# Two more column pairs in layer 1's front, attention steps at half quarters, conditioning spread in layer 0

## The chip, the cores and the metric

The kernel runs on one core of a Trainium2 chip. The metric is the device time of one execution in microseconds. The version before has a median of 2278.35 us over three runs (2276.54 to 2283.84).

The engines go by their names in the profile: PE is TensorE (PEld its weight loads), DVE is VectorE, ACT is ScalarE, POOL is GpSimd, SP is SyncE, which here only issues DMAs.

## The reference: what is computed

Two layers of a diffusion trunk over 640 tokens, 512 latent and 128 context ones, model width 2048. For each layer:

```
h = rmsnorm(x) * (1 + scale) + shift          # shift, scale, gate = silu(cond) @ ada_w + ada_b
p = h @ w_in                                  # split into columns, see below
y = concat(branch1 * silu(gate1), branch2 * silu(gate2))
x = x + gate * (y @ w_out)
```

Layer 0 has windowed attention with a sink and a gated width-3 convolution. Layer 1 has *differential* attention (four heads, two softmax maps each, `cq`, `ck`, `cv`, gates `cg`) and *dense* attention (eight query heads over two key/value heads, `dq`, `dk`, `dv`, gates `dg`). Queries and keys are normalised per head, and for latent tokens rotated. Latent queries see 256 cached keys as well. New keys and values of the context tokens are outputs (`new_d_k`, `new_d_v` for the dense branch). The conditioning `silu(cond) @ ada_w` is a product with two columns (context and latent).

## The kernel before, in words

**Matrix products.** Activations lie transposed, 16 blocks of 128 rows by 640 tokens. All big products are done in three parts, high x high, high x low and low x high, of operands split into a rounded part and its remainder (`split`, L291: ScalarE copies the high part, L292; VectorE subtracts, L293). A *column tile* is 128 output columns over the 640 tokens, two halves of 320. `proj_q` (L320) does one *quarter* of it, four row blocks: 4 x 3 x 2 = 24 matmuls (L327 to L329), first half `pa`, then half `pb`.

**Column pairs.** `run_pairs` (L519) takes two column tiles together, with a two-by-two block scheme of seven products instead of eight (M1, M5, M6, M2, M7, M3, M4 in this order). Each product is half a tile's rows by half its tokens: 8 row blocks x 3 = 24 matmuls (L612 to L614, PSUM tile `pq`), so a pair has 168, and two tiles have 192. It needs sums of weight blocks (VectorE, L551 to L563) and of activations (`forms`, L1133, made once per stage and kept as `T`). There are two `slot` calls in each product, one after its first half and one at its end.

**Slots.** `run_tiles` (L379) goes through a list of jobs, each a column tile and the function that takes its result. Weights are loaded five quarters ahead (`RAW_AHEAD`) and split three ahead (`SPLIT_AHEAD`). After each quarter comes one `slot` (L367), which gives one step to each of the generators in `prep` (what is done with finished tiles: `q_gen` L723, `k_gen` L656, `v_gen` L770), `steps` steps to the first generator in `attn` (attention, or `forms`), and `rate` steps to the `fill` generator (conditioning products on VectorE). So the source writes the order by hand; the builder may still move an instruction among those of its engine where its operands allow, and allots buffers from pools.

**Attention steps.** `pair_gen` (L878 is its product with the values) works on two heads and five blocks of 128 queries, in twelve steps: a score with its softmax (L827 to L829 into `S`; L789 to L796; normalising L890), the transposes of an earlier block's weights (L815), and their product with the values. The one `S` tile takes two PSUM banks. `diff_gen` (from L1527) has fourteen steps per head.

**Conditioning.** Layer 0's conditioning partly runs on TensorE. The rest are the multiply-adds of `ada_wide` (L258), `ada_slow` (L270, L279, L281; loads by POOL into one place in `tables`) and `ada_on_dve` (L206, L216, L218; loads by SP). Each ends in a fold on TensorE (`ada_fold`, L224). `fill0b`, an `ada_slow` over two blocks of 512 columns, runs at 0.33 steps a slot in layer 0's pairs; a step is one weight tile, two multiply-adds. `fill1`, an `ada_on_dve` over four blocks in halves of 256 columns, runs at 1.3 steps a slot in layer 1's tiles.

**Order of stages.** Layer 0: lead tiles and 28 tiles with windowed attention; six more tiles from `n_turn` on, beside which `forms` runs at 0.4 steps a quarter; nine pairs of the convolution's columns. Then the output projection. Layer 1's *front*: six gate tiles, then eight pairs (eight gates, eight `cv` tiles), whose results go to DRAM (`gdram`, `vdram`; `value_rows`, L1625, turns values into rows). Then the pool `odd` opens and 30 tiles follow: dense attention's queries, keys and values (12 jobs, at one step a quarter), differential queries and keys (16, at 1.1 steps from job 13 on), and two gates. Then the output projection.

Of the kernel before, what the change touches and what calls it, by code (L numbers as in the profile page):

```python
# [11 lines left out]
F32 = mybir.dt.float32  # L12
# [8 lines left out]
P = 128  # L21
# [30 lines left out]
FILL1 = 1.3  # L52
# [4 lines left out]
def trunk_kernel(ctx: ExitStack, tc: tile.TileContext, I: dict, O: dict):  # L57
# [133 lines left out]
    def ada_on_dve(blocks, tags, parts=1, tie=lambda: None):  # L191


        wt, wd = tags[2:5], 512 // parts
        bufs = 3 if wt[0] == wt[1] else 1
        for l, cb in blocks:
            ap = pools["cur"]
            acc = [ap.tile([P, 512], F32, tag=tags[c], name=f"acc{c}", bufs=1) for c in range(2)]
            mark = tie()
            if mark is not None:  # L200
                for c in range(2):
                    V.tensor_copy(acc[c][:, 0:1], mark)
            def fetch(i):
                kt, c0 = i % KT, cb * 512 + i // KT * wd
                w = ap.tile([P, wd], F32, tag=wt[i % 3], name="adaw", bufs=bufs)
                nc.sync.dma_start(w, I["ada_w"][l, kt * P:(kt + 1) * P, c0:c0 + wd])  # L206
                return w

            nxt = fetch(0)
            for i in range(KT * parts):  # L210
                kt, h = i % KT, i // KT
                w, nxt = nxt, (fetch(i + 1) if i + 1 < KT * parts else None)
                for c in range(2):
                    a = acc[c][:, h * wd:(h + 1) * wd]
                    if kt == 0:
                        V.tensor_scalar(a, w, sT[:, kt, c:c + 1], None, ALU.mult)  # L216
                    else:
                        V.scalar_tensor_tensor(out=a, in0=w, scalar=sT[:, kt, c:c + 1], in1=a,  # L218
                                               op0=ALU.mult, op1=ALU.add)
                yield  # L220
            ada_fold(l, cb, acc, ap, tags[5], 3 if tags[5] == wt[0] else 1)
            yield
# [42 lines left out]
    def ada_slow(blocks):  # L265

        w = tables[:, 3 * HALF:3 * HALF + 512]

        def fetch(l, cb, kt):
            nc.gpsimd.dma_start(w, I["ada_w"][l, kt * P:(kt + 1) * P, cb * 512:(cb + 1) * 512])  # L270

        fetch(*blocks[0], 0)
        yield
        for b, (l, cb) in enumerate(blocks):
            acc = [xr_tile(f"acc{c}")[:, 0:512] for c in range(2)]
            for kt in range(KT):
                for c in range(2):
                    if kt == 0:
                        V.tensor_scalar(acc[c], w, sT[:, kt, c:c + 1], None, ALU.mult)  # L279
                    else:  # L280
                        V.scalar_tensor_tensor(out=acc[c], in0=w, scalar=sT[:, kt, c:c + 1], in1=acc[c],  # L281
                                               op0=ALU.mult, op1=ALU.add)
                if kt + 1 < KT:
                    fetch(l, cb, kt + 1)
                elif b + 1 < len(blocks):
                    fetch(*blocks[b + 1], 0)
                yield
# [78 lines left out]

    def slot(fill=None, rate=0.0, steps=1.0):  # L367
        settle_late()
        advance(prep, len(prep))
        pace[0] += steps  # L370
        while pace[0] >= 1.0:
            advance(attn, 1)
            pace[0] -= 1.0
# [5 lines left out]
    def run_tiles(jobs, w_ap, make_h, fill=None, rate=0.0, ahead=None, order=(0, 1, 2, 3), before=None,  # L379
# [89 lines left out]
        for i in range(lead, len(jobs)):  # L469
            fn = jobs[i][1]  # L470
            if turn and i == turn[0]:
                drain(prep)
                turn[1]()
                rate = 0.0
# [13 lines left out]
            for qd in range(4):  # L488
                proj_q(pp, parts[t], qd, qd, HV[:1] if split_last else HV)
# [7 lines left out]
                slot(fill, rate if t > fill_from else 0.0, steps(i))  # L497
# [21 lines left out]
    def run_pairs(cols, w_ap, mov, room, used, begin, done, tail, fill=None, rate=0.0):  # L519
# [82 lines left out]
        for i, (p, name) in enumerate(seq):  # L602
# [5 lines left out]
            for h in range(2):  # L608
# [7 lines left out]
                if h == 0:  # L616
                    ahead(2 * i + 1)
                    slot(fill, rate)
# [11 lines left out]
            slot(fill, rate)  # L630
# [25 lines left out]
    def k_gen(ap, pp, tag, src, gain, new_out, vals=None, then=None):  # L656
# [9 lines left out]
        x = stage(ap, pp)  # L666
# [5 lines left out]
        junk = ap.tile([P, P * st["sets"]], F32, tag="junk", name="junk", bufs=1)[:, 0:P]  # L672
# [22 lines left out]
        V.tensor_mul(y, x, cosR[:, :, None, :].to_broadcast([P, 8, 2, 32]))  # L695
# [1125 lines left out]
```

## Time and profile before

| | |
|---|---|
| median of three runs | 2278.35 us |
| the profiled execution, its time | 2275.12 us |
| its span (first to last instruction) | 2273.3 us |
| PE, DVE, ACT, POOL busy | 98%, 75%, 49%, 10% of the span |
| mean granted clock of TensorE | 0.996 |
| moved by DMA | 351.43 MB, mean 155 GB/s |

"Busy" joins the spans of an engine's instructions. A matmul's span is a model, longer than its share of the array, so busy does not mean at its peak. A wait row reads: who, of which line, waited for which engine's tile and line; then us in all, times, and the longest. A row of the stage table (from:to, length) gives busy us and count for each engine. The chain of work that ended last has 50% on PE, 6% on DVE, 3% on ACT.

### The profile page before, as it was taken

Reading aid. Unit: us, or ns where it says so; the run is one execution under the profiler, and the core shown is the slowest. Engines: PE = TensorE matmul, PEld = TensorE weight load, DVE = VectorE, ACT = ScalarE, POOL = GpSimd, SP = SyncE. Lnnn points to the kernel's source line nnn. Section 1 sums busy time; section 2 is a strip of 40 time slices with the busy share of each in tenths; the row PEclk is TensorE's granted clock in tenths of the full one; section 3 lists DMA queues with packets and bytes.
Section 4 is the critical chain, followed back from the end, with each engine's and each line's share of the span. In section 5 each row is a group of like instructions: output and inputs, shape, how many; then the busy total and the mean of one; then the engine's idle time right before and its main releaser. Section 6 shows DMA issues by size and latency. Waiting matters only on the chain.

```text
span 2273.3 us, 41407 instructions
## 1 busy us (share of the span) xinstructions
PE 2230.9 (98%) x15708; PEld 2156.4 (95%) x15708; DVE 1712.6 (75%) x3197; ACT 1109.6 (49%) x2293; POOL 225.3 (10%) x337
## 2 busy tenths in 40 slices
PE   7999999999999999999999999999999999999999
PEld 5889999999999999999999999999999999999999
DVE  4659899988868898887776764858658778676665
ACT  4335554544333435444644445566665554554443
POOL 2220000000001000000200000010010111111010
PEclk9999999999999999999999999999999999999999
DMA  9985556564534447743763334423324234237541
GB/s 357 340 284 156 175 171 204 164 188 151 157 100 130 135 122 227 210 140 113 246 211 115 108 110 141 132 71 99 94 76 145 76 115 131 78 114 245 168 134 49
DMA packets 385607, 351.43 MB, mean 155 GB/s; under 512 B 18162, under 2 KB 342224, under 8 KB 384896
## 3 DMA queue, kind: packets, MB, share of 16 engines
q1 hardware_dynamic: 369008, 289.76, 42.5%
q0 software_dynamic: 15536, 56.80, 7.2%
q8 instruction: 123, 2.02, 0.4%
q10 hardware_dynamic: 864, 2.23, 0.3%
q14 instruction: 76, 0.62, 0.1%
HBM read 305.86 MB, written 42.86 MB: 153 GB/s over the span
## 4 chain that ended last, share of the span: by engine, by line
PE 50%; DVE 6%; ACT 3%; issue 2%; DMA 2%; POOL 1%; ACTq 0%; DVEq 0%; POOLq 0%; SPq 0%
PE pq L612 8%; PE pq L613 8%; PE pq L614 8%; PE pb L328 3%; PE pb L327 3%; PE pa L329 3%; PE pb L329 3%; PE pa L328 3%; PE pa L327 3%; DVE acc L218 1%; PE T L642 1%; PE T L815 1%; DMA adaw<-in_ada_w 1%; DVE nm L789 1%; ACT p L796 1%
## 5 line engine op out<-in xcount | busy, mean ns | idle before, releaser
L292 ACT ACTIVATE wh<-raw 128x512 fp32r<-128x512 f32 (+1 forms) x400 | 241.1, 604 | 393.5 <-PE pb L328 277.3
L327 PE MATMUL pa<-h,wh 128*128 128x320 f32 x1216 | 388.7, 320 | 0.4 <-DVE sum L416 0.4
L328 PE MATMUL pa<-h,wh 128*128 128x320 f32 x1216 | 379.0, 312 | 1.5 <-DVE h L293 1.5
L327 PE MATMUL pb<-h,wh 128*128 128x320 f32 x1216 | 378.1, 311 | 0.9 <-ACT h L292 0.9
L329 PE MATMUL pa<-h,wl 128*128 128x320 f32 x1216 | 377.9, 311 | 0.0
L329 PE MATMUL pb<-h,wl 128*128 128x320 f32 x1216 | 377.8, 311 | 0.0
L328 PE MATMUL pb<-h,wh 128*128 128x320 f32 x1216 | 377.4, 310 | 0.0
L293 DVE TENSOR_TENSOR wl<-raw,wh 128x512 fp32r<-128x512 f32 (+1 forms) x400 | 261.2, 654 | 142.2 <-ACT wh L292 126.5
L612 PE MATMUL pq<-h,wh 128*128 128x320 f32 x896 | 277.4, 310 | 0.0
L614 PE MATMUL pq<-h,wl 128*128 128x320 f32 x896 | 277.1, 309 | 0.0
L613 PE MATMUL pq<-h,wh 128*128 128x320 f32 x896 | 276.6, 309 | 0.0
L327 PEld LDWEIGHTS pa<-h,wh 128*128 128x128 f32 x1216 | 228.9, 188 | 10.6 <-issue 9.7
L328 PEld LDWEIGHTS pa<-h,wh 128*128 128x128 f32 x1216 | 229.3, 189 | 6.5 <-issue 4.5
L327 PEld LDWEIGHTS pb<-h,wh 128*128 128x128 f32 x1216 | 229.5, 189 | 2.1 <-ACT h L292 1.1
L329 PEld LDWEIGHTS pa<-h,wl 128*128 128x128 f32 x1216 | 228.8, 188 | 1.6 <-issue 1.6
L328 PEld LDWEIGHTS pb<-h,wh 128*128 128x128 f32 x1216 | 229.4, 189 | 0.4 <-issue 0.4
L329 PEld LDWEIGHTS pb<-h,wl 128*128 128x128 f32 x1216 | 229.2, 188 | 0.4 <-issue 0.4
L612 PE MATMUL pq<-T,wh 128*128 128x320 f32 x672 | 209.3, 311 | 3.4 <-ACT wh L292 1.8
L614 PE MATMUL pq<-T,wl 128*128 128x320 f32 x672 | 208.3, 310 | 2.7 <-DVE wl L293 2.7
L613 PE MATMUL pq<-T,wh 128*128 128x320 f32 x672 | 208.2, 310 | 0.0
L258 DVE SCALAR_TENSOR_TENSOR acc<-adaw,sT,acc 128x1024 f32<-128x1024 f32 x150 | 189.1, 1275 | 0.0
L292 ACT ACTIVATE wh<-sx 128x512 fp32r<-128x512 f32 x168 | 105.1, 632 | 151.7 <-PE pq L613 96.2
(375 smaller groups left out, 4682.7 us busy)
## 6 DMA issues: line engine op xcount, KB each, us to landing
adaw<-in_ada_w SPq DMA_DIRECT2D x80, 512.0 KB, 4.0
raw<-in_od_w_in SPq DMA_DIRECT2D x160, 256.0 KB, 3.0
raw<-in_ev_w_in SPq DMA_DIRECT2D x130, 256.0 KB, 3.5
ada<-in_ada_w SPq DMA_DIRECT2D x11, 2048.0 KB, 13.5
adaw<-in_ada_w SPq DMA_DIRECT2D x128, 128.0 KB, 2.4
w<-in_ev_w_in SPq DMA_DIRECT2D x27, 512.0 KB, 3.9
w<-in_od_w_in SPq DMA_DIRECT2D x24, 512.0 KB, 4.0
adah<-in_ada_w SPq DMA_DIRECT2D x20, 512.0 KB, 9.2
```

Source lines behind the costliest of these rows:

```text
L218: V.scalar_tensor_tensor(out=a, in0=w, scalar=sT[:, kt, c:c + 1], in1=a, op0=ALU.mult, op1=ALU.add)
L258: V.scalar_tensor_tensor(out=acc[c], in0=w, scalar=sT[:, kt, c:c + 1], in1=acc[c], op0=ALU.mult, op1=ALU.add)
L292: A.activation(hi, x, AF.Copy)
L293: V.tensor_sub(lo, x, hi)
L327: PE.matmul(ps, wh[:, i, :], hi[:, sl], start=(j == js[0] if alone else (pos == 0 and j == 0)), stop=False)
L328: PE.matmul(ps, wh[:, i, :], lo[:, sl], start=False, stop=False)
L329: PE.matmul(ps, wl[:, i, :], hi[:, sl], start=False, stop=(j == js[1] - 1 if alone else (pos == 3 and j == 3)))
L612: PE.matmul(ps, wh[:, j, :], hi, start=(first and h == 0 and j == 0), stop=False, skip_group_check=True)
L613: PE.matmul(ps, wh[:, j, :], lo, start=False, stop=False, skip_group_check=True)
L614: PE.matmul(ps, wl[:, j, :], hi, start=False, stop=(final and h == 1 and j == 3), skip_group_check=True)
L642: PE.transpose(t[:, i * P:(i + 1) * P], src(b), ident)
L789: V.tensor_reduce(nm, s, axis=AX.X, op=ALU.max, negate=True)
```

## The change

- `dk` and `dv` (two tiles each) leave the odd stage's job list and are appended to the front as two more pairs, ahead of `cv`: `key_out` copies a key tile to SBUF and stores it in `kdram`; values go the way of `cv`, `value_rows`, to `vdram` and `new_d_v`.
- In the odd stage `keys_first` reads both key tiles back and runs `k_gen` on them, two steps a slot, beside the first tile. `with_values` loads and splits the dense values ahead of a pair's first step.
- `pace_attn`: half of a quarter's attention steps are now counted after the first half (`pa`) of the quarter, the other half at its end. Dense queries' and the next tiles (jobs 2 to 9) run at 1.5 steps a quarter, later ones at 1.1.
- `ada_slow` yields after each multiply-add instead of two, keeps two loads ahead (in `w8` tiles, later in two alternating places), starts in the six tiles of layer 0 at 0.7 steps a slot, and in the pairs moves only in the products M6, M2 and M3, one step a slot.
- `ada_on_dve` works on 512 columns instead of 256, with two buffers instead of three; `FILL1` goes from 1.3 to 0.85.
- Two scratch tiles (`junk`) become bf16, and a small tile of the lambda computation is reused.

```diff
-FILL1 = 1.3
+FILL1 = 0.85
...
     def ada_slow(blocks):
-        w = tables[:, 3 * HALF:3 * HALF + 512]
-        def fetch(l, cb, kt):
+        todo = [(l, cb, kt) for l, cb in blocks for kt in range(KT)]
+        places, ws = [], []
+        def fetch():
+            if not todo:
+                return
+            l, cb, kt = todo.pop(0)
+            if "adaw" in st:
+                w = st["adaw"]()
+            else:
+                if not places:
+                    places.extend([tables[:, 3 * HALF:3 * HALF + 512], xr_tile("adaw")[:, 0:512]])
+                w = places[0]
+                places.reverse()
             nc.gpsimd.dma_start(w, I["ada_w"][l, kt * P:(kt + 1) * P, cb * 512:(cb + 1) * 512])
...
+                    if c:
+                        ws.pop(0)
+                        fetch()
+                    yield
...
+    def pace_attn(steps):
+        pace[0] += steps
+        while pace[0] >= 1.0:
+            settle_late()
+            advance(attn, 1)
+            pace[0] -= 1.0
...
-                proj_q(pp, parts[t], qd, qd, HV[:1] if split_last else HV)
+                if split_last:
+                    proj_q(pp, parts[t], qd, qd, HV[:1])
+                else:
+                    proj_q(pp, parts[t], qd, qd, HV[:1])
+                    pace_attn(steps(i) / 2)
+                    proj_q(pp, parts[t], qd, qd, HV[1:])
...
-                slot(fill, rate if t > fill_from else 0.0, steps(i))
+                slot(fill, rate if t > fill_from else 0.0, steps(i) / 2)
...
-                    slot(fill, rate)
+                    slot(fill, float(name in rests))
...
+    def with_values(values, ap, width, k, *rest):
+        rows_, src = values
+        raw = ap.tile([P, 5, P], F32, tag="ctxv", name="vrow", bufs=1)
+        ctx_ = ap.tile([P, 2, P], F32, tag="ctxk", name="vctx", bufs=1)
+        nc.sync.dma_start(raw.rearrange("p b f -> p (b f)"), rows_)
+        nc.sync.dma_start(ctx_, src.rearrange("(c p) d -> p c d", p=P))
+        yield
+        hi, lo = st["v"] = tuple(ap.tile([P, 7, P], F32R, tag=t, name=t) for t in ("vh", "vl"))
+        split(hi[:, 2:7, :], lo[:, 2:7, :], raw)
+        split(hi[:, 0:2, :], lo[:, 0:2, :], ctx_)
+        yield from pair_gen(ap, width, k, st["v"], *rest)
...
-                     turn=(n_turn, tail_turn), twist=twist, fill_from=FILL0_FROM)
+                     turn=(n_turn, fill0b, 0.7, tail_turn), twist=twist, fill_from=FILL0_FROM)
...
-              fill0b, 0.33)
+              fill0b, ("M6", "M2", "M3"))
...
+    def key_out(j):
+        x = xr_tile("kx")
+        def put(t, sl, src):
+            A.copy(x[:, sl], src)
+            if (j, "k") in half_done:
+                nc.gpsimd.dma_start(kdram[j], x)
+            half_done.add((j, "k"))
+        return put
...
-            + [OD["cv"] + i * P for i in range(8)], N_FRONT, h1_maker,
+            + [OD[n] + i * P for n, m in (("dk", 2), ("dv", 2), ("cv", 8)) for i in range(m)], N_FRONT, h1_maker,
...
-        if n % 2 == 0:
-            jobs.append((OD["dk"] + kv * P, k_job(f"k{kv}", I["cache_d_k"][0, 0, kv], "d_k_norm", O["new_d_k"][0, 0, kv])))
-            jobs.append((OD["dv"] + kv * P, v_job(I["cache_d_v"][0, 0, kv], O["new_d_v"][0, 0, kv], then)))
+        jobs.append((OD["dq"] + (h + 1) * P, q_job("q1", "d_q_norm", then)))
+    def keys_first():
+        for kv in range(2):
+            yield from k_job(f"k{kv}", I["cache_d_k"][0, 0, kv], "d_k_norm", O["new_d_k"][0, 0, kv])(kdram[kv])
...
-    brisk.update((i, 1.1) for i in range(13, len(jobs)))
+    brisk.update((i, 1.5 if i < 10 else 1.1) for i in range(2, len(jobs)))
```

More of the change, by code (lines that the diff above doesn't have):

```diff
@@ L629, in run_pairs @@
                 tail(name)
-            slot(fill, rate)
+            slot(fill, float(name in rests))
     def stage(ap, pp):
@@ L665, in k_gen @@
         nc.sync.dma_start(raw, src.rearrange("(c p) d -> p c d", p=P))
-        x = stage(ap, pp)
+        if isinstance(pp, tuple):
+            x = stage(ap, pp)
+        else:
+            x = ap.tile([P, NT], F32, tag="stg", name="kx", bufs=2)
+            nc.sync.dma_start(x, pp)
         if vals:
@@ L928, in trunk_kernel @@
     fill0b = ada_slow([(1, 2), (1, 3)])
[L929 to L930 removed]
+    fill1 = ada_on_dve([(1, cb) for cb in range(8, 12)])
     ydram = [dram.tile([P, NT], F32, name=f"yd{k}") for k in range(KT)]
     x0dram = [dram.tile([P, 4 * NT + 1], F32, name=f"x0d{g}") for g in range(4)]
+    kdram = [dram.tile([P, NT], F32, name=f"kd{k}") for k in range(2)]
     xdram, hdram, gdram, vdram = ([dram.tile([P, NT], F32, name=f"{n}{k}") for k in range(KT)]
@@ L1512, in odd_start @@
         V.tensor_reduce(ls, lp, axis=AX.X, op=ALU.add)
-        le = small.tile([P, 2], F32, tag="le", name="le", bufs=1)
+        le = ls
         A.activation(le, ls, AF.Exp)
```

87 lines of the change are left out of this document (42 added, 45 removed).

## The prediction

> **What bounds the kernel now.** I read the head of the page first, then TensorE's timeline, the table by stage, and the waits.
>
> ```profile
> span 2273.3 us, 41407 instructions
> ...
> PE 2230.9 (98%) x15708; PEld 2156.4 (95%) x15708; DVE 1712.6 (75%) x3197; ACT 1109.6 (49%) x2293; POOL 225.3 (10%) x337
> ```
>
> TensorE is the bound, but the 0.31 us that a matmul shows is not its price, since neighbours overlap. The price is the distance of two starts. In the timeline of one quarter of a column tile:
>
> ```profile
> 600.62 0.31 PE L327 MATMUL pa<-h,wh 128*128 128x320 f32 x1
> ...
> 604.14 0.31 PE L327 MATMUL pa<-h,wh 128*128 128x320 f32 x1
> ```
>
> From the first row to the second lie 24 matmuls (four row blocks, three products, two halves) and 3.52 us: **0.1467 us each**. A quarter is 3.52 us, half a quarter 1.76, a column tile (96 matmuls) 14.08.
>
> Then by stage. First TensorE's pair products alone, in layer 0's nine pairs and in layer 1's eight front pairs:
>
> ```profile
> 653.30:887.00 233.70, 226.44 (x1512) 0.99 0.45 134
> 1188.60:1389.40 200.80, 198.62 (x1344) 1.00 0.36 108
> ```
>
> Then all engines (PE, PEld, DVE, ACT, POOL busy; granted clock, DMA share, GB/s), in the six tiles ahead of layer 0's pairs, in those pairs, and in the odd stage's start, its dense attention, and the start of differential attention:
>
> ```profile
> 562.20:653.30 91.10, 91.10 (x630) 89.89 (x629) 65.24 (x114) 31.80 (x55) 3.24 (x6) 1.00 0.44 131
> 653.30:887.00 233.70, 227.56 (x1534) 223.98 (x1534) 203.18 (x327) 100.60 (x179) 18.83 (x35) 0.99 0.45 134
> 1389.40:1462.00 72.60, 71.45 (x493) 69.76 (x492) 48.47 (x108) 31.06 (x70) 7.93 (x10) 1.00 0.54 166
> 1462.00:1690.00 228.00, 225.85 (x1604) 217.76 (x1604) 149.08 (x328) 148.41 (x296) 16.97 (x17) 1.00 0.28 85
> 1690.00:1755.00 65.00, 61.89 (x432) 60.18 (x431) 50.08 (x119) 32.78 (x79) 6.72 (x9) 0.97 0.45 136
> ```
>
> The front pairs are clean: 1344 x 0.1467 = 197.2 of 200.8 us, and the other 3.6 hold the values' transposes. Layer 0's pairs are not: 1512 x 0.1467 = 221.8 of 233.7 us. I estimate 2 us for the 22 matmuls of the conditioning folds (1534 less 1512), which leaves **9.9 us lost**. TensorE's waits there (all four rows: us, times, longest), and the longest of VectorE's, say by what:
>
> ```profile
> PE pq L614 <- DVE wl L293: 2.7, 3, 1.3
> PE pq L612 <- ACT wh L292: 1.8, 3, 0.9
> PE pq L612 <- ACT tables L581: 1.0, 1, 1.0
> PE pq L612 <- DVE tables L591: 0.6, 1, 0.6
> ```
>
> ```profile
> DVE acc L281 <- DMA tables<-in_ada_w: 18.7, 19, 2.2
> ```
>
> VectorE is 87% busy there (203.18 of 233.70) and besides sits 18.7 us waiting for conditioning weights, in front of the splits that TensorE needs. TensorE's rows name 6.1 of the 9.9 us; the rest I put to the clock (1% of 233.7 us is 2.3) and short gaps.
>
> **The change part by part.**
>
> *Four tiles become two pairs.* Removed: 4 x 96 = 384 tile matmuls. Added: 2 x 168 = 336 pair matmuls. 48 x 0.1467 = **7.0 us less**, which nothing can hide, since TensorE is without slack in both stages. The transposes of keys and values and the copies out of PSUM are as many as before. The two new pairs should lose as little as the eight beside them: VectorE and ScalarE have room there, and if not, 9.9 / 9 = 1.1 us each, as in layer 0. The new traffic (two key and two value arrays of 320 KB, out and back) meets a DMA that is 28% to 54% busy, and its readers come over 40 us later: nothing. The Trainium skill ("TensorE: Matmul & The Clock Gate", Back-to-back issue gap) gives about 81 ns per matmul for 128 columns and 131 for 512 in a stream of weight loads and matmuls; for 320 I estimate 106 from that page, and the saving would be 5.1 us. The trace's 146.7 ns disagrees, and I go by it.
>
> *Conditioning in layer 0.* One multiply-add of this generator, and its load:
>
> ```profile
> L281 DVE SCALAR_TENSOR_TENSOR acc<-tables,sT,acc x60: 741/746/756, 663.2 to 847.7; 128x512 f32<-128x512 f32 x60
> ```
>
> ```profile
> tables<-in_ada_w POOLq DMA_DIRECT2D x32, 256.0 KB, 3.1
> ```
>
> Now 64 of them (60 and the four firsts) run two at a time, 9.2 per pair (14 slots x 0.33 x 2), from one buffer: the next load, 3.1 us, starts only when both are done. After the change there are two loads ahead; about 16 move into the six tiles (24 slots x 0.7), the others come singly, six per pair, only in M6, M2 and M3. Per pair VectorE loses 3.2 x 0.746 = 2.4 us of work and 18.7 / 9 = 2.1 us of waiting, out of 26.0 us. It should then keep up as in the front: I take **8 of the 9.9 us**; the ends are 0 and 9.9. The loads stay on POOL's queue, some 90 us earlier; behind them stand stores that nobody reads before the next projection.
>
> The moved steps cost 16 x 0.746 = 12 us of VectorE in the six tiles, whose 91.1 us hold 65.24, unevenly:
>
> ```profile
> 590.00:600.00 10.00, 10.00 (x70) 10.00 (x69) 9.95 (x17) 4.45 (x7) 0.00 (x0) 1.00 0.41 121
> 630.00:640.00 10.00, 10.00 (x70) 10.00 (x69) 2.92 (x5) 2.30 (x5) 0.00 (x0) 1.00 0.30 87
> ```
>
> VectorE is full at 590 and idle at 630; TensorE is full in both. Splits are made three quarters (10.6 us) ahead, which covers nearly all of a delay of 12 us spread over 24 quarters: 0, at worst 2 us.
>
> *Odd stage: denser attention.* Dense attention keeps its 48 steps, with two more that only load, but has eight column tiles beside it and not twelve: 1.5 steps a quarter from the third tile, none two without half a quarter between them. TensorE's tile matmuls from 1462 to 1690, first and second half:
>
> ```profile
> 1462.00:1690.00 228.00, 77.69 (x461) 1.00 0.28 85
> ```
>
> ```profile
> 1462.00:1690.00 228.00, 75.41 (x468) 1.00 0.28 85
> ```
>
> 929 x 0.1467 = 136.3 us, so 33 steps (one exponential each, below) with the query sums take 91.7: 2.8 us a step. The distance of steps falls from 3.52 + 2.8 = 6.3 us to 3.52 / 1.5 + 2.8 = 5.1, at least 1.76 + 2.8 = 4.6. What must fit in is a softmax chain, and on ScalarE what a query tile puts beside it (shortest/median/longest in ns):
>
> ```profile
> L796 ACT ACTIVATE p<-S,nm,rq x33: 453/992/999, 1462.8 to 1685.2; 128x768 f32<-128x768 f32 x27, 128x128 f32<-128x128 f32 x6
> L796 ACT ACTIVATION_READ_ACCUMULATOR p<-S,nm,rq x33: 188/191/212, 1463.7 to 1686.1; 128x1 f32 x33
> L890 ACT ACTIVATE p<-p,rl x33: 399/933/942, 1464.9 to 1687.2; 128x768 f32<-128x768 f32 x27, 128x128 f32<-128x128 f32 x6
> ```
>
> ```profile
> L791 DVE TENSOR_SCALAR nm<-nm,rq x33: 202/208/216, 1462.5 to 1683.6; 128x1 f32<-128x1 f32 x33
> L789 DVE TENSOR_REDUCE nm<-S x32: 278/950/958, 1465.6 to 1682.1; 128x1 f32<-128x768 f32 x26, 128x1 f32<-128x128 f32 x6
> ```
>
> ```profile
> L731 ACT COPY qsw<-qx x32: 614/617/621, 1471.4 to 1684.5; 32x512 f32<-32x512 f32 x32
> L727 ACT ACTIVATE qx<-pa,vec x8: 508/522/537, 1468.4 to 1680.2; 128x320 f32<-128x320 f32 x8
> ```
>
> ```profile
> L728 ACT ACTIVATE qsq<-pa x8: 423/432/438, 1469.7 to 1681.5; 128x320 f32<-128x320 f32 x8
> ```
>
> Reduce 0.95, scaling the maximum 0.21, exponential 0.99 + 0.19, reciprocal of one column (0.2, taken from the scaling beside it), normalising 0.93: 3.5 us. That fits into 4.6, but not right behind a query tile, which puts 4 x 0.617 + 2 x 0.522 + 2 x 0.432 = 4.4 us on ScalarE. ScalarE goes from 65% (148.41 of 228) to some 80% (65 x 6.3 / 5.1). Against this, waits go. TensorE's longest from 1389 to 1755 (all of them make 6.1 us), and VectorE's for its conditioning weights:
>
> ```profile
> PE T L642 <- DVE k1l L293: 2.9, 1, 2.9
> PE T L642 <- DVE k0l L293: 1.1, 1, 1.1
> PE T L878 <- DVE y L1068: 1.1, 1, 1.1
> ```
>
> ```profile
> DVE acc L218 <- DMA adaw<-in_ada_w: 8.9, 11, 3.6
> ```
>
> At 1.3 steps a slot with one load ahead, two steps sometimes fall into one slot and VectorE stands for the load, ahead of the key splits (`k0l`, `k1l`). At 0.85 two never do, and the work per slot stays, 1.3 x 2 x 0.477 against 0.85 x 2 x 0.746 us, the first by this row:
>
> ```profile
> L218 DVE SCALAR_TENSOR_TENSOR acc<-adaw,sT,acc x240: 460/477/486, 1421.9 to 1915.5; 128x256 f32<-128x256 f32 x120
> ```
>
> So I take back the two key waits, 4 us, and let the denser steps cost 4, half a microsecond for each of the eight query tiles: **0**. The ends: 6 us better (all waits) and 22 worse (below).
>
> The dense keys' generators run at double speed in the first tile and end some 20 us before the first score. Their loads are new in SP's queue at the change of pools, with weight loads behind them. There the order is already favourable:
>
> ```profile
> 1387.06 8.48 SPq L305 DMA_DIRECT2D raw<-in_od_w_in  x4
> 1395.60 0.50 SPq L1507 DMA_DIRECT2D lam<-in_c_lambda  x1
> ```
>
> Four weight loads go out before the first load into the new pool, so I cost it at 0; without that cover one load, 3.1 us, would be late once.
>
> **Sum:** -7.0 - 8 + 0 = -15 us. The profiled execution took 2275.12 us, 1.8 more than its span, and would become 2260. The median of the runs shown, 2278.35, is 3.2 above it; from that, **2263 us**.
>
> **The rivals.**
>
> *Slower: the softmax chain becomes the bound.* If behind each of the eight query tiles ScalarE's 4.4 us stand ahead of an exponential, what does not fit is 4.4 - (5.1 - 3.5) = 2.8 us each, 22 in all, and the sum is +7: 2285. It decides from 15 / 8 = 1.9 us a tile. For it: ScalarE at 80%, and one score tile in PSUM. Against: at one step a quarter the same burst leaves TensorE no wait over 1.1 us in dense attention (the 2.9 is a differential key's), so the burst has gone through slack before. Chance 0.09. The Trainium skill (the same page, Architectural detail) has ScalarE and VectorE as strict FIFOs; by that rule a burst delays every exponential queued behind it. The 2.9 us wait of TensorE behind VectorE agrees.
>
> *The pairs alone.* Layer 0's pairs stay as they are, because the splits are late for their own operands' sake, or the moved steps hold up the six tiles: -7.0, 2271, from 2267 to 2276. For it: the named waits, 6.1 us, are fewer than the loss. Against: the front's pairs, with the same operands, lose nothing. Chance 0.19.
>
> *More.* All 9.9 us and the odd stage's 6 go: -23, 2255, from 2250 to 2258. Chance 0.13; it needs the denser steps for nothing.
>
> **How the numbers follow.** The forecast (-10 to -20 us, 2258 to 2268) has the remaining 0.59. About 0.3%, 6.8 us, is what a measurement of this kernel can tell: 2271.5. Faster: 0.59 + 0.13 + 0.07 of the pairs alone = 0.79; the other 0.12 of that case are within 0.3%; slower 0.09. The range of 8 in 10 takes the forecast, most of the pairs alone and most of the richer case: 2253 to 2275.
>
> **What would show it.** The front's `pq` must count 1344 + 336 = 1680, in some 251 us (246.5 and 4.6 of transposes). Layer 0's pairs should last 224 to 227 us, with VectorE's wait for `in_ada_w` under 4 us; the six tiles keep 91 us. Dense attention shows ScalarE near 80% and TensorE's waits of at most 6 us up to the first differential key. I am wrong if layer 0's pairs last over 230 us, or if `S` and `T` matmuls wait above 12 us between the front and differential attention.

## The result and the profile after

The changed kernel takes **2271.95 us** (median of 7 runs, 2268.14 to 2274.38) where the kernel before takes 2278.73 us on the same chip (7 runs, 2276.54 to 2283.84): ratio 0.9968, 95% interval [0.9959, 0.9978], 6.8 us less. The forecast was 15 us less. The profiled execution took 2270.89 us. The head of its page:

```profile
span 2269.1 us, 41048 instructions
...
PE 2226.5 (98%) x15660; PEld 2147.9 (95%) x15660; DVE 1720.0 (76%) x3093; ACT 1121.4 (49%) x2313; POOL 226.2 (10%) x341
```

48 matmuls fewer, as counted. The table by stage (from:to, length, then busy us and count of PE, PEld, DVE, ACT, POOL; clock, DMA share, GB/s), for layer 0's pairs and the front's pairs:

```profile
655.70:881.40 225.70, 224.06 (x1534) 222.31 (x1533) 190.60 (x301) 100.77 (x177) 12.91 (x24) 1.00 0.41 122
...
1182.10:1433.20 251.10, 251.10 (x1726) 251.05 (x1726) 164.94 (x242) 122.69 (x236) 15.02 (x28) 1.00 0.36 109
```

Layer 0's pairs went from 233.7 to 225.7 us. Their waits, VectorE's for the conditioning weights, then all of TensorE's:

```profile
DVE acc L287 <- DMA adaw<-in_ada_w: 2.4, 1, 2.4
```

```profile
PE pq L626 <- ACT wh L297: 1.0, 1, 1.0
PE pq L628 <- DVE wl L298: 0.6, 1, 0.6
```

VectorE's 18.7 us of waiting became 2.4, TensorE's 6.1 became 1.6. Both steps up to here came out as worked out.

Now the odd stage, in three parts: the dense tiles and the first four differential ones (sixteen tiles before, twelve after), the next sixteen (twelve differential tiles, two gates, two of the output projection), and four more of the output projection. Of before:

```profile
1389.40:1732.90 343.50, 340.01 (x2406) 328.80 (x2404) 231.44 (x516) 203.81 (x421) 29.63 (x33) 1.00 0.35 106
1732.90:2079.60 346.70, 338.39 (x2351) 325.22 (x2350) 255.69 (x566) 176.78 (x433) 50.90 (x77) 1.00 0.38 116
```

```profile
2079.60:2139.10 59.50, 58.97 (x407) 58.50 (x406) 42.37 (x79) 23.92 (x42) 6.45 (x10) 1.00 0.80 246
```

Of after:

```profile
1433.30:1724.30 291.00, 285.33 (x1996) 270.35 (x1995) 201.34 (x400) 189.25 (x392) 27.91 (x30) 1.00 0.36 111
1724.30:2072.40 348.10, 338.95 (x2361) 324.86 (x2360) 257.46 (x526) 178.54 (x436) 50.56 (x77) 1.00 0.38 115
```

```profile
2072.40:2134.80 62.40, 60.55 (x412) 58.85 (x411) 44.73 (x84) 24.20 (x42) 6.46 (x10) 1.00 0.81 253
```

The first part lost four tiles, 4 x 14.08 = 56.3 us, and 1.1 us of the values' transposes that now stand in the front; it became only 52.5 us shorter. The second grew by 1.4, the third by 2.9. **Of 57.4 us the stage kept back 9.2.** (A few transposes moved across the cuts between the parts, five of them into the last; the 9.2 us of the whole stage do not depend on this.) TensorE's waits in the first part name little of it:

```profile
PE T L656 <- DMA kx<-kd: 1.9, 1, 1.9
PE S L846 <- ACT p L815: 1.2, 2, 0.8
PE T L656 <- DVE kg L706: 0.9, 1, 0.9
PE T L898 <- DVE ptl L298: 0.8, 2, 0.6
```

A stop under some 0.2 us gets no row. So I also reckoned from the starts in the trace: the distance from each matmul to the next, less what the same neighbours take at their closest, summed by the kind that comes next (us). `T` is the PSUM tile of the transposes, among others. Transposed into it are, for keys: `kx` (a dense key read back), `stg` (a key or value straight from its column tile), `ctxk` (cached keys), `kg` (normalised) and `m` (rotated); and for attention: `p` (softmax weights) and `on` (the result of differential attention). A second profile of each unaltered kernel tells what is chance:

| odd stage | before | before, again | after | after, again |
|---|---|---|---|---|
| all of it | 749.7 | 748.9 | 701.5 | 703.7 |
| first part, beyond its tiles' 14.08 us each | 118.1 | 118.3 | 122.0 | 123.5 |
| next sixteen tiles, beyond | 121.4 | 120.5 | 122.8 | 122.9 |
| last four, beyond | 3.2 | 3.1 | 6.0 | 6.6 |
| first part: late before scores `S` | 2.3 | 3.1 | 5.8 | 6.6 |
| first part: before `T` of `kx`, `ctxk`, `kg` | 0.0 | 0.0 | 3.9 | 3.8 |
| first part: before `T` of `m` and `stg` | 2.2 | 1.5 | 0.0 | 0.0 |
| sixteen: before `T` of `p` | 2.5 | 2.5 | 7.8 | 7.7 |
| sixteen: before `T` of `on` and `m` | 9.1 | 8.7 | 3.3 | 3.3 |

In the sixteen tiles one wait takes the place of others. What is lost lies, by the means of two profiles, at the scores (3.5 us), at the dense keys (3.8) and in the last four tiles (3.2), against 1.9 of waits that went; small ones make the rest. The forecast had put all of this together at 0.

### The profile page after: what moved, and what is told of

Read it like the earlier page. It is cut to its first block, busy times and chain, and to the rows that moved or that the text cites. A ratio compares the mean times of both kernels' runs of the same rounds, so it can differ in the third digit from the quotient of the medians.

```text
span 2269.1 us, 41048 instructions
## 1 busy us (share of the span) xinstructions
PE 2226.5 (98%) x15660; PEld 2147.9 (95%) x15660; DVE 1720.0 (76%) x3093; ACT 1121.4 (49%) x2313; POOL 226.2 (10%) x341
## 4 chain that ended last, share of the span: by engine, by line
PE 80%; DVE 6%; DMA 6%; ACT 4%; issue 3%; POOL 1%; SPq 0%; DVEq 0%; ACTq 0%; POOLq 0%
PE pq L626 10%; PE pq L628 10%; PE pq L627 10%; PE pa L332 6%; PE pa L333 6%; PE pb L332 6%; PE pb L333 6%; PE pb L334 6%; PE pa L334 6%; PE T L834 2%; DMA adaw<-in_ada_w 1%; DVE wl L298 1%; PE S L846 1%; PE T L656 1%; PE T L178 1%
## 5 line engine op out<-in xcount | busy, mean ns | idle before, releaser
L332 PE MATMUL pa<-h,wh 128*128 128x320 f32 x1152 | 367.3, 319 | 0.2 <-DVE sum L425 0.2
L333 PE MATMUL pa<-h,wh 128*128 128x320 f32 x1152 | 359.6, 312 | 0.9 <-DVE h L298 0.9
L332 PE MATMUL pb<-h,wh 128*128 128x320 f32 x1152 | 359.6, 313 | 0.9 <-ACT h L297 0.9
L334 PE MATMUL pb<-h,wl 128*128 128x320 f32 x1152 | 358.0, 311 | 0.7 <-DVE wl L298 0.7
L333 PE MATMUL pb<-h,wh 128*128 128x320 f32 x1152 | 358.4, 311 | 0.0
L334 PE MATMUL pa<-h,wl 128*128 128x320 f32 x1152 | 358.1, 311 | 0.0
L626 PE MATMUL pq<-h,wh 128*128 128x320 f32 x960 | 297.7, 310 | 0.0
L627 PE MATMUL pq<-h,wh 128*128 128x320 f32 x960 | 296.6, 309 | 0.0
L628 PE MATMUL pq<-h,wl 128*128 128x320 f32 x960 | 296.4, 309 | 0.0
L332 PEld LDWEIGHTS pa<-h,wh 128*128 128x128 f32 x1152 | 216.9, 188 | 11.4 <-issue 10.3
L626 PE MATMUL pq<-T,wh 128*128 128x320 f32 x720 | 223.5, 310 | 1.0 <-ACT wh L297 1.0
L628 PE MATMUL pq<-T,wl 128*128 128x320 f32 x720 | 222.6, 309 | 0.6 <-DVE wl L298 0.6
L333 PEld LDWEIGHTS pa<-h,wh 128*128 128x128 f32 x1152 | 217.1, 188 | 6.1 <-issue 4.8
L627 PE MATMUL pq<-T,wh 128*128 128x320 f32 x720 | 222.4, 309 | 0.0
L332 PEld LDWEIGHTS pb<-h,wh 128*128 128x128 f32 x1152 | 217.8, 189 | 2.1 <-ACT h L297 1.1
L333 PEld LDWEIGHTS pb<-h,wh 128*128 128x128 f32 x1152 | 217.5, 189 | 1.2 <-issue 1.2
```

Of the source, the lines that this page charges most:

```text
L332: PE.matmul(ps, wh[:, i, :], hi[:, sl], start=(j == js[0] if alone else (pos == 0 and j == 0)), stop=False)
L333: PE.matmul(ps, wh[:, i, :], lo[:, sl], start=False, stop=False)
L334: PE.matmul(ps, wl[:, i, :], hi[:, sl], start=False, stop=(j == js[1] - 1 if alone else (pos == 3 and j == 3)))
L626: PE.matmul(ps, wh[:, j, :], hi, start=(first and h == 0 and j == 0), stop=False, skip_group_check=True)
L627: PE.matmul(ps, wh[:, j, :], lo, start=False, stop=False, skip_group_check=True)
L628: PE.matmul(ps, wl[:, j, :], hi, start=False, stop=(final and h == 1 and j == 3), skip_group_check=True)
```

## The experiments

Theory A: denser steps make the scores wait for the one `S` tile. Theory B: the coarser conditioning steps make VectorE late. Theory K: the keys' loads and their chain are late at the stage's start. Theory N: it is chance. Each kernel was compared with the kernel before on its own chip; us are medians.

**Layer 0 alone (e1), and all but layer 0 (e2).** e1 is the kernel before with the new `ada_slow`, its start in the six tiles and its three products; e2 the changed kernel with these as before (`fill0b, 0.33`).

> The kernel before with the conditioning part of the change alone (one multiply-add per step, loads ahead, started in the six tiles, only in M6, M2, M3). Theory A (the layer 0 part gives its 8 us by itself, the other parts cost what they bring): layer 0's pairs last 225 to 227 us, the six tiles are unchanged, and the whole is 6 to 9 us faster than before. Rival B (the moved steps are paid elsewhere, in the six tiles or the next stage): pairs as in A, but the whole at most 5 us faster.

> The changed kernel with layer 0's conditioning as before; keys, values, attention steps and layer 1's conditioning stay changed. Theory A (the odd stage gives back what the two pairs save): layer 0's pairs 233 to 234 us, the odd stage about 701 us, the whole within 3 us of before. Rival B (the pairs' 7 us arrive and something in layer 0 is lost): 5 to 8 us faster than before.

e1: 2270.85, ratio 0.998 [0.9969, 0.999], 5.1 us less. e2: 2279.31, 1.0014 [1.0005, 1.0022], 3.3 us more. Layer 0's pairs took 225.2 us in e1 and 234.2 in e2. So the whole gain is layer 0's: 5.1 us alone, some 10 as the difference of the changed kernel and e2. The rest of the change costs time.

In e1 the pairs are 8.3 us shorter and the whole only 5.1, for its odd stage grew, though its source there is that of the kernel before. That stage, and its longest TensorE wait in the last four tiles, for which the profile shows no releaser:

```profile
1380.10:2134.70 754.60, 736.88 (x5158) 710.85 (x5158) 529.66 (x1158) 404.78 (x895) 85.44 (x119) 1.00 0.40 121
```

```profile
PE T L654 <- issue: 2.5, 1, 2.5
```

It took 754.6 us, 5.3 more than the mean of two profiles of before (749.3), 3.3 of them in the last four tiles. What differs is the order that was built: from the stage's start on, 299 of the 6051 places in TensorE's order hold another matmul than before, and none does in the second profile of before. So there is a rival to all theories above, call it O: another order of the same work can move this stage by some 5 us. Against e1's stage the changed kernel keeps back not 10.7 us (the means below) but 5.4. No run separates the two. That something is kept back holds without it: the fifteen builds with the pairs moved took 699.6 to 710.2 us there, and 749.3 - 57.4 is 691.9.

**Steps at quarter ends (e3).**

```diff
-                    proj_q(pp, parts[t], qd, qd, HV[:1])
-                    pace_attn(steps(i) / 2)
-                    proj_q(pp, parts[t], qd, qd, HV[1:])
+                    proj_q(pp, parts[t], qd, qd, HV)
```

> The changed kernel with attention steps at quarter ends alone: at 1.5 a quarter every second quarter has two in a row. Theory A (the denser steps are what costs, and half quarters soften it): dense attention 3 to 10 us longer than in the changed kernel. Rival B (the order that is built already spreads the work, so places in the source hardly matter): within 2 us of the changed kernel.

2272.32, 0.9985 [0.9976, 0.9994]; the odd stage took 702.4 us, the scores were late by 6.9. Half quarters neither cause the loss nor cure it. (By the ratios e3 is 2 to 4 us slower than the changed kernel; the odd stage does not show where.)

**The keys' steps one slot later (e4):** one `yield` ahead of `in_twos`' loop.

> The changed kernel with the dense keys' generator held back by one slot at the odd stage's start, so that TensorE reaches their transposes when the load has landed. Theory A (about 3 us of the odd stage's loss are its start): the 1.9 us wait of the transposes for kx is gone and the whole is 2 to 3 us faster than the changed kernel. Rival B (dense steps alone): within 1 us of it, with the wait moved.

2269.61, 0.9975 [0.9965, 0.9984]. The transposes stood at the same place in TensorE's order, behind 75 matmuls of the stage, and waited 2.28 us for `kx`: one slot later in the source did not move them in the order that was built. The expected gain did not come; the run served as one more of the changed kernel.

**The changed kernel again (after_again), and the kernel before again (before_again).**

> The changed kernel once more, unaltered, for a second profile of identical work and as the base on this chip. All theories: 0.996 to 0.998 of the kernel before. What its stages differ in from the first profile of the same kernel is the noise of one profile: theory N (noise) expects the excess of dense attention, of differential attention and of the last four tiles to move by 1 to 3 us each; theories A and B expect A's 122 and B's 122 us (excess over the tile matmuls) again, within 1 us.

> The kernel before, unaltered, for a second profile of it: 1.000. Theory N (the first profile of before was a lucky one in the odd stage, 749.7 us, and its last four tiles lost 3.2 us where five other kernels lose 5.7 to 7.9): the odd stage takes 752 to 755 us here, the last four tiles lose 5 to 7 us, and the change's true loss in the odd stage is 2 to 4 us smaller than the two first profiles say. If the first profile was typical: 749 to 751 us.

2273.08, 0.9967 [0.9954, 0.9979]; and 2279.30, 0.9996 [0.9985, 1.0007]. Their stages are in the table above: the odd stage repeats within 0.8 us before and 2.2 after. Theory N falls; the 749.7 us was no lucky profile.

**Layer 1's conditioning as before (e7), and the pairs' move alone (e8).** e7 has the old `ada_on_dve`, 256 columns, at 1.55 steps a slot; e8 adds e2's and e3's edits to it; the denser steps beside eight tiles stay, and so do small parts of the change (the bf16 scratch tiles, one more `yield` in the rotation of keys).

> The changed kernel with layer 1's conditioning multiply-adds as before (halves of 256 columns, three buffers; 1.55 steps a slot, since there are fewer slots). Theory B (steps of 512 columns, 0.75 us on VectorE and not 0.48, delay the mix of differential attention, for which the transposes then wait): that wait falls from 7.8 to about 4 us and the time by 3 to 4 us. Theory A (the softmax chain is what the denser steps wait for) and my forecast (the coarse steps take the waits for conditioning weights away): no gain, or 1 to 4 us slower, and a wait of the key splits for these loads comes back.

> The move of the two pairs alone: the changed kernel with layer 0's conditioning, layer 1's conditioning and the place of the attention steps (quarter ends) all as before. The forecast's sum gives -7 us by the pairs. Theory A (denser dense attention, key loads at the odd stage's start and denser differential attention take about as much as the pairs give): -2 to +3 us against before, the front 251 us, the odd stage some 702 us. Theory B (the loss comes from the coarser conditioning steps): -5 to -7 us, the odd stage under 698 us.

e7: 2273.89, 0.9976 [0.9966, 0.9987]. The wait before `p` fell only to 6.2 us and the time not at all: theory B in this form is out. e8: 2281.74, 1.0004 [0.9994, 1.0013]: **moving the pairs, with the denser steps that it brings, is worth nothing by itself.** Its front took 251.2 us, as forecast; its odd stage 704.8.

**The kernel before, only denser (e11).**

```diff
-    brisk.update((i, 1.1) for i in range(13, len(jobs)))
+    brisk.update((i, 1.5 if i < 13 else 1.1) for i in range(2, len(jobs)))
```

> The kernel before with only the pace changed: dense attention's steps at 1.5 a quarter beside its twelve tiles, as in the changed kernel, and no pair moved. Theory A (denser steps cost TensorE waits, above all the scores on the one S tile): the waits before scores in dense attention rise from 0 to 1 us to 3.5 to 5.5 us, as in the changed kernel, and the time by 3 to 5 us, 1.0015 to 1.002 of before. My forecast (no cost at this density) and theory K (what is lost is lost at the keys' loads): the same time, within 1 us, scores as before.

2288.12, 1.0037 [1.0022, 1.0053], 8.6 us more. TensorE's longest waits in its first part:

```profile
PE T L642 <- DVE k0l L293: 3.7, 2, 2.0
PE T L642 <- DVE k1l L293: 1.6, 1, 1.6
PE T L706 <- DVE kg L678: 1.0, 1, 1.0
```

The same work, put closer, costs what theory A said and more. But by kinds only 2.6 us of it stand before scores; 6.9 before key transposes (`m`, `kg`, `ctxk`), which wait for VectorE; and 3.0 in the last four tiles, where e1 lost as much without a change of pace. The denser steps hit the keys above all. In the changed kernel these keys are out of the way, but at another place.

**Is it ScalarE's burst (e5)? VectorE's conditioning (e6)?** e5 puts the rotation copies on POOL; e6 starts layer 1's conditioning behind dense attention.

```diff
-            A.copy(sw[32 * d:32 * d + 32, :], x[32 * (d ^ 1):32 * (d ^ 1) + 32, 0:NS])
+            G.tensor_copy(sw[32 * d:32 * d + 32, :], x[32 * (d ^ 1):32 * (d ^ 1) + 32, 0:NS])
```

```diff
-FILL1 = 0.85
-FILL1_FROM = 8
+FILL1 = 1.15
+FILL1_FROM = 44
```

> The changed kernel with the four rotation copies of each query tile (4 x 0.617 us) on POOL, not ScalarE, in both layers. The form of theory A that my rival named (ScalarE's burst of 4.4 us behind a query tile stands ahead of an exponential, and the score waits for the S tile): scores' waits fall from 5.8 to 6.6 us to about 3 and the time by 2 to 4 us. If the score waits for something else than ScalarE's burst: scores' waits as in the changed kernel, the time within 1.5 us of it.

> The changed kernel without layer 1's conditioning beside dense attention (it starts at the 45th quarter, at 1.15 steps a slot and not 0.85). If VectorE's work is what makes the denser softmax late (its reduce and scaling stand behind multiply-adds of 0.75 us): scores' waits in dense attention fall from 5.8 to 6.6 us to 2 to 3 and dense attention's excess by 3 to 5 us, while differential attention's rises by 1 to 4. If the chain itself is the cost: scores' waits as they are, dense attention's excess within 1.5 us, the time the same or up to 4 us slower by differential attention.

e5: 2285.95, 1.0029 [1.0017, 1.0042]. In the odd stage nothing moved (702.9 us, scores late by 6.2): the burst that my slower rival named is not what the scores wait for. The time went in layer 0's tiles (629.1 us, not 617 to 619), by a wait there that the changed kernel has no row for. I take it that slow copies cause it, since one takes up to 2.8 us on POOL, with a median of 0.61 (shortest/median/longest in ns); no run shows this by itself:

```profile
PE S L846 <- ACT p L815: 7.6, 4, 3.2
```

```profile
L750 POOL COPY qsw<-qx x32: 599/612/2825, 183.4 to 504.1; 32x512 f32<-32x512 f32 x32
```

e6: 2277.88, 0.9991 [0.998, 1.0002]. The first part's excess fell to 119.4 us (by 2.7 to 4.1), the scores' share to 4.8; the next sixteen tiles rose by 11, where the conditioning now stood ahead of the differential keys:

```profile
PE T L656 <- DVE k1l L298: 6.0, 4, 4.1
```

VectorE's load seems to be part of the density's price (1 to 2 us before scores, from one profile), and the place before was the better one.

**Dense attention over ten tiles (e16):** `1.25 if i < 12` for `1.5 if i < 10`.

> The changed kernel with attention's steps from the third to the twelfth tile at 1.25 a quarter, not 1.5 in eight of them and 1.1 in two: the same work over ten tiles. Theory A (the density of steps is what costs: 8.6 us in the kernel before, where only the pace was raised): the scores' and values' waits fall, the odd stage loses 2 to 4 us less, 0.995 to 0.996 of before. If what is lost is lost at the keys' loads and in differential attention: the same time, or up to 2 us slower, as the last dense pair ends later.

2272.62, 0.9972 [0.9962, 0.9981]. Nothing gained: scores and products with the values were late by 17.1 us over both parts, against 16.7 and 17.2. Between 1.25 and 1.5 steps density does not decide; theory A's expectation is missed. Why the scores lose 3.5 us more than before is settled only in part, by e6.

**The start of the odd stage (e9, e14, e15, e18, e19).** SP's issues in the changed kernel, then the stage table there, then the same place of the kernel before:

```profile
1430.87 8.48 SPq L310 DMA_DIRECT2D raw<-in_od_w_in  x4
1439.40 0.50 SPq L1541 DMA_DIRECT2D lam<-in_c_lambda  x1
1439.95 0.42 SPq L1553 DMA_DIRECT2D con<-in_c_out_norm  x1
1440.42 0.43 SPq L679 DMA_DIRECT2D ctxk<-in_cache_d_k  x1
1440.95 0.89 SPq L684 DMA_DIRECT2D kx<-kd  x2
```

```profile
1434.00:1438.00 4.00, 4.00 (x30) 3.82 (x29) 0.69 (x1) 1.51 (x5) 1.07 (x2) 1.00 0.96 314
1438.00:1442.00 4.00, 4.00 (x29) 4.00 (x28) 0.96 (x2) 0.86 (x2) 0.00 (x0) 1.00 0.50 170
1442.00:1446.00 4.00, 2.41 (x17) 2.14 (x15) 1.59 (x5) 0.20 (x1) 0.00 (x0) 1.00 0.93 267
```

```profile
1398.00:1402.00 4.00, 4.00 (x29) 4.00 (x28) 2.02 (x7) 0.73 (x2) 0.00 (x0) 1.00 0.88 272
```

The four weight loads that I took for a cover hold SP for 8.5 us, since each waits for a split on VectorE to free its buffer, by SP's row there:

```profile
SPq L310 <- DVE wl L298: 8.5, 5, 3.7
```

The keys stand behind them, the last of a burst of loads with the DMA engines at 96%, 50% and 93%. Before, the burst is as dense (88%), but nothing needs a load at once: 29 matmuls in 4 us, where there are now 17. e9 lets POOL issue the keys' loads:

```diff
-            nc.sync.dma_start(x, pp)
+            nc.gpsimd.dma_start(x, pp)
```

> The changed kernel with the two loads of the dense keys issued by POOL, not by SP behind four weight loads. If the first transposes wait for these loads because of SP's order: the load lands some 5 us earlier, TensorE's wait for it, 1.9 to 2.3 us, goes, and the time falls by up to 2 us; dense attention's excess falls from 122 to 120 us. If the wait is only moved to the next late operand (the conditioning of the pool change, the transposes of the next key): the same time.

e14 lets POOL issue the loads of `lam4`, `con` and the cached keys too, ahead of the keys:

> The changed kernel with all of the odd stage's first loads (lambda, its norm, the dense keys and their cached parts) issued by POOL and not by SP behind four weight loads, so that neither the key transposes nor ScalarE's exponential of lambda, ahead of the keys' squares in its queue, waits for them. Theory K (the changed kernel's loss at the start of the odd stage is SP's order and the chain behind it): the waits before the transposes of kx, ctxk and kg, 3.7 to 4 us together, fall below 1 us, and the time by 3 to 4 us, to 0.995 of before. Theory A: the loss lies later, in scores; at most 1 us here.

e9: 2272.70, 0.9966 [0.9954, 0.9978]; e14: 2273.64, 0.9974 [0.9962, 0.9986]. No gain. In e9 `kx` was there in time and the next transposes waited:

```profile
PE T L725 <- DVE kg L696: 3.5, 1, 3.5
```

Three of the key's five squares (L694) stood in ScalarE's queue behind lambda's exponential, which waited 3.36 us for its own load and sums:

```profile
1441.78 0.19 ACT L694 ACTIVATION_READ_ACCUMULATOR junk<-T 128x1 f32 x1
1445.33 0.20 ACT L1548 ACTIVATE ls<-ls 128x2 f32<-128x2 f32 x1 [3.36 <-DVE ls L1546]
1445.44 0.26 ACT L694 ACTIVATE junk<-T 128x128 bf16<-128x128 f32 x1
```

In e14 the median `kx` load took 7.8 us behind the other loads:

```profile
kx<-kd POOLq DMA_DIRECT2D x2, 320.0 KB, 7.8
```

So SP's order alone is not the cause: there is a whole burst of loads, and behind it a chain of four engines. So e15 loads the keys first, values behind them, all by POOL, and makes lambda twelve slots later:

```diff
     open_pool("odd")
-    odd_start()
+    def lambda_later():
+        for _ in range(12):
+            yield
+        odd_start()
...
     prep.append(in_twos(keys))
+    prep.append(lambda_later())
```

> The changed kernel with the dense keys' loads first at the odd stage's start: their loads, those of the cached keys and of the dense values go by POOL, in this order, and lambda's load, sums and exponential come twelve slots later, out of ScalarE's queue there. Theory K (at that place the DMA engines are full for some 14 us, and the key chain waits for its own place among the loads, by whichever queue): TensorE's waits before the transposes of kx, ctxk and kg, 3.7 to 4.6 us in all four kernels before this one, fall to under 2 us, and the time by 2 to 3 us, to 0.9955 of before. If the transposes are merely placed earlier and wait again: the same time, within 1 us of the changed kernel.

2271.60, 0.9964 [0.9949, 0.9978]: the rival's case. The transposes were set 11 matmuls earlier, and their chain was late for the next ones (`ctxk`, 2.0 us). e18 ties the first key to a weight split further on, and e19 joins e15 and e18; e17 joins e15 and e16.

```diff
+        if not isinstance(pp, tuple) and tag == "k0":
+            for _ in range(6):
+                yield
+            V.scalar_tensor_tensor(out=x[:, 0:1], in0=mark[0], scalar=0.0, in1=x[:, 0:1], op0=ALU.mult, op1=ALU.add)
```

> The two edits of e15 and e16 together. If both causes stand and lie at different places, the gains add up: 4 to 7 us less than the changed kernel, 0.994 of before. If they share one slack: no more than the better of the two.

> The changed kernel with the first dense key's transposes tied to a weight split some three quarters into the stage (a first column of the key has nought times a column of that split added), so that they stand 26 matmuls, 3.8 us, later in TensorE's order, behind the landing of their load, while the first score stands where it stood. Theory K: the waits before the transposes of kx, ctxk and kg fall from 3.8 to 3.9 us to 1 to 2.5, and the time by 1.5 to 3 us, to 0.9955 to 0.996 of before. Rival G (what is gained early is given back at the end of the stage, where the residual's rows come by a DMA that is 81% busy): the waits fall as said, the last four tiles lose as much more, and the time stays within 1 us of the changed kernel.

> The edits of e15 (keys' loads first, lambda later) and of e18 (first key's transposes tied later) together. Theory K: next to nothing is left of the waits before kx, ctxk and kg (0.5 to 2 us of 3.8 to 3.9), the time 2 to 3 us under the changed kernel, 0.995 to 0.996 of before. Rival G: the waits fall as said, the time stays within 1 us of the changed kernel.

e17: 2272.15, 0.9965 [0.9953, 0.9977], nothing added. e18: 2270.49, 0.997 [0.9959, 0.9982]: late at the keys by 3.3 us, not 3.8, the time unchanged. e19: **2267.31, 0.9955 [0.9944, 0.9967]**, the fastest version. TensorE's waits in its first part:

```profile
PE S L850 <- ACT p L819: 2.2, 4, 0.9
PE T L656 <- DVE kg L710: 1.6, 2, 0.9
PE T L902 <- DVE ptl L298: 0.2, 1, 0.2
```

Of the keys' waits only `kg` is left in the rows; by starts they are still 2.6 us, where 0.5 to 2 were expected. The first part is beyond its tiles by 120.6 us, not 122.0 to 123.5, and the odd stage took 699.6. This fits theory K, early loads and later transposes together, but does not prove it. The step from 0.9967 to 0.9955 is about 2.7 us, as expected, but the intervals overlap, and the waits that went are only 1.2 us of it. The last four tiles lost 5.3 us, no more than in the changed kernel, so rival G is not shown.

## Why the prediction was off: point by point

- *Four tiles become two pairs, -7.0 us:* right. 1680 `pq` in 251.1 us, 50.3 more than before (49.3 forecast for the matmuls, the rest transposes).
- *Conditioning in layer 0, -8 us:* right. The pairs are 8.0 us shorter in the first profiles (by rows), 7.7 between the means of two. VectorE's wait is 2.4 us, under the 4 named; the tiles ahead took 619.5 and 616.8 us, 617.0 and 621.7 before: no cost to be seen.
- *Odd stage, 0 us:* **this step failed.** It measures +9.2 us by the first profiles; by the means of two the stage became 749.3 - 702.6 = 46.7 us shorter and not 57.4, +10.7. Three terms under it failed. The keys' loads, put at 0, or 3.1 us for one late load: 3.8 us, for the load and the chain behind it. Two terms that were not in my sum at all: in the sixteen tiles, the transposes of `p` became 5.2 us later, which used up what went before `on` and `m`; and the last four tiles lost 3.2 us more, before transposes of the residual, at a DMA share of 0.81. There e14 and e15 were over by only 3.1 and 3.4, as before, and e1 by 6.5 without an edit in this stage. What sets these two places stays open, and some 2 us lie in small stops. The terms that I did have, -4 + 4, came out nearly: the two key waits of my rows are gone (`k0l`, 1.1, in the first part, and `k1l`, 2.9, in the sixteen tiles), and the scores cost 3.5 more. How much of the 10.7 is the change's and how much the order that was built (theory O, 5.3 us in e1) is not shown.
- *The sum:* -7.0 - 7.7 + 10.7 is -4.0, where the medians and the spans' means (2275.5 and 2268.7) both say -6.8. The 2.8 us between lie in stages whose work is the same, the kernel's start, layer 0's tiles and the front's tiles, about 1.2 us in each; layer 0's tiles alone scatter by 4.7 us between two profiles of one kernel. I do not count them as the change's.
- *The rival "softmax chain":* its place was right in part (scores, 3.5 of its 22 us), its mechanism wrong. ScalarE is 71% busy in dense attention (147.22 of 208.40 us from the first score on), not 80%, and taking its burst away changed nothing (e5). The row (ScalarE is the fourth engine):

```profile
1481.60:1690.00 208.40, 205.93 (x1442) 194.81 (x1441) 155.33 (x309) 147.22 (x283) 14.17 (x13) 1.00 0.32 96
```

- *The rival "the pairs alone"* had its time nearly (2271) for the opposite reason: layer 0 gave its part, the pairs gave theirs away.
- *What I said would show it:* waits of at most 6 us in dense attention. The rows add up to 4.8, and the first part still lost 3.8 us more than before. Rows of waits are no measure of many small stops; the length of the stage against its matmuls is.

For the keys, my argument went wrong at one place in the table by stage: a DMA share of 0.28 to 0.54 over 70 to 230 us was read as room at the stage's first 15 us, where it is 0.85. It was 0.84 there before, too; what is new is a load that TensorE needs at once.

## What to carry to other kernels

When work leaves a stage that is bound by one engine, what stays moves closer together: cost the stage that is left by raising its pace in the old kernel, alone, before counting the removed work as won. Where operands that a stage made itself are now loaded at its start, look at the DMA share of that very place, at what else opens there, and at every engine of the chain from the load to the first use; an earlier load and a later use may each be worth nothing, and something together. Compare stage lengths against counted matmuls, in two profiles of each kernel, since waits below a fraction of a microsecond have no row. And look also at stages that were not edited: here one moved by 5 us, in another order of the same work.

## What the runs showed of the hardware

A stop of TensorE can cost twice. In the second profile of the changed kernel (start, duration, instruction; idle before it in brackets), around the wait for `kx`:

```profile
1441.08 0.31 PE L332 MATMUL pb<-h,wh 128*128 128x320 f32 x1
1443.35 1.27 PE L656 MATMUL T<-ident,kx 128*128 128x128 f32 x5 [1.96 <-DMA kx<-kd]
1444.27 0.61 PE L333 MATMUL pb<-h,wh 128*128 128x320 f32 x1
1444.68 0.47 PE L334 MATMUL pb<-h,wl 128*128 128x320 f32 x1
```

```profile
1440.00:1444.00 4.00, 2.04 (x14) 0.92 0.95 299
1444.00:1448.00 4.00, 4.00 (x21) 0.65 0.56 203
1448.00:1452.00 4.00, 4.00 (x31) 1.00 0.87 271
```

Behind a wait of 1.96 us the granted clock (third figure from the end) was 0.65 for 4 us, and 21 matmuls ran where 31 ran next. Cut at its edges, the slow stretch is 3.4 us at 0.50. The kernel before has the same in its first profile, behind the wait of 2.9 us for `k1l`, and not in its second, behind 2.8 us:

```profile
1443.39:1446.79 3.40, 3.40 (x14) 0.50 0.77 289
```

```profile
1749.83:1753.23 3.40, 3.40 (x15) 0.50 0.45 127
1753.30:1756.70 3.40, 3.40 (x24) 1.00 0.29 86
```

The same followed waits of 2.0 to 3.5 us in e8, e9, e14 and e15 (0.50 to 0.68 over 3 us), but not those of 2.0 to 2.6 us in e2, e3 and e7. The Trainium skill ("TensorE: Matmul & The Clock Gate", Part 1: The HAM clock gate) has the clock halve after an idle window of some 3.4 us, free-running; the halving agrees, but here waits of 2 us were enough at times. So the same wait weighs differently from one execution to the next. Ten matmuls fewer are 1.5 us by the distance of 0.1467 us, which is what the first part's 122.0 and 123.5 us differ by. In the odd stage each kernel has one such stretch in its two profiles, so the means of two carry it alike.
